# The low part of some weight pieces made by an adding DMA in place of a VectorE subtraction

## The chip, the cores and the metric

The kernel runs on one core of a Trainium2 chip. The metric is the device time of one execution in microseconds (us), the median of several runs. The engines of the core are named as in the profile: PE (TensorE, with PEld for its weight loads), DVE (VectorE), ACT (ScalarE), POOL (GpSimd) and SP (SyncE, which here only issues DMAs).

## What is computed

One decoder layer in float32 on 256 tokens of width 2048: a SwiGLU feed-forward, a token mixer (selected sparse attention beside a gated recurrence), and a second feed-forward, with a layer norm after each. The change is in the feed-forwards' input product `h @ w_in`:

```
D_MODEL = 2048
SEQ = 256
D_FF = (8 * D_MODEL // 3 + 255) // 256 * 256
...
def swiglu(h, w_in, w_out):
    a, b = jnp.split(h @ w_in, 2, axis=-1)
    return (jax.nn.silu(a) * b) @ w_out
...
h = layer_norm(DN_ALPHA * h + 0.5 * swiglu(h, ffn1_w_in[l], ffn1_w_out[l]), ln1_g[l], ln1_b[l])
...
h = layer_norm(DN_ALPHA * h + merged @ w_out[l], ln2_g[l], ln2_b[l])
h = layer_norm(DN_ALPHA * h + 0.5 * swiglu(h, ffn2_w_in[l], ffn2_w_out[l]), ln3_g[l], ln3_b[l])
```

`D_FF` is 5632, so `w_in` is 2048 x 11264.

## The kernel before

**Split operands.** TensorE multiplies in the rounded type `float32r`. So every operand is split into a high part h (the value rounded, by ScalarE, line 157) and a low part l = w - h (by VectorE, line 158), and a product is three matmuls: xh with wh, xh with wl, xl with wh (`three`, lines 521 to 523). The weights are streamed once, and each must be loaded, split and used.

**Pieces.** All weights form one list of pieces, in the order in which TensorE uses them. A piece is 128 partitions by 1024 columns (`PIECE`). Class `Weights` walks this list with three cursors: `load_to` issues the loads on SP's queue, `split_to` makes h and l, `unit` hands the columns to TensorE. Each time TensorE's program comes to a new piece, `unit` calls `load_to` for up to `AHEAD + LOADS` = 4 + 5 pieces ahead and `split_to` for up to `AHEAD` = 4 pieces ahead, and makes one step of the background work (`bg.step`: gates, norms, row loads). This sets the program's order alone. In time, what holds loads and splits back are the buffers: a plain piece is loaded into one of five raw buffers (tag `raw`), which is free again when its split is done, and h and l of each piece lie in one of five pairs (tags `wh`, `wl`, `HL_BUFS`), which is free when TensorE has used it. PE, SP and POOL run in the order of the program; the order on DVE and ACT is planned by the framework's scheduler.

**Blocks of the input product.** A feed-forward's input product has 22 blocks of 512 columns (256 of a, 256 of b), in three segments of 8, 8 and 6 (`SEGS`). After each segment comes the output product of its columns (32, 32 and 24 plain pieces). The first block of each feed-forward is made of 8 plain pieces (`PLAIN_PLAN`). The other 21 follow `FAST_PLAN`, 12 pieces: in each half of the block a plain piece ("c"), then two pieces of a fast product (a Strassen-like scheme with sums of weights), a second plain piece, and two more fast pieces:

```
c  p1q3  p2  c  q5p7  q4p6   c  p1q3  p2  c  q5p7  q4p6
```

A plain piece is 12 matmuls of 512 columns; p2 is 6 matmuls of 256 columns, the other three are 12 of 256 columns each (`blockF`). The four fast pieces of a half are made from one load of 1 MB (tag `rf`, two buffers) by sums on VectorE (`operand`, lines 128, 132 and 135); the last of them, q4p6, frees the rf buffer.

**Gates.** At a block's end, `gate` forms silu(a) * b in a buffer z (two of them); eight pieces later (four at a segment's end) TensorE transposes it (line 758).

**POOL** does little: the row loads of the norms' gains and biases (line 486), a few small instructions of the norms, and the low parts of eight pieces just ahead of the first two norms (`W.spare`).

Of the kernel before, what the change touches and what calls it, by code (L numbers as in the profile page):

```python
# [8 lines left out]
F32 = mybir.dt.float32  # L9
F32R = mybir.dt.float32r  # L10
I32 = mybir.dt.int32
AF = mybir.ActivationFunctionType
OP = mybir.AluOpType
AX = mybir.AxisListType.X

P = 128
# [28 lines left out]
for _k, _w in (("ln1_g", NK), ("ln1_b", NK), ("ln2_g", NK), ("ln2_b", NK), ("conv_w", 4 * NR),  # L45
# [5 lines left out]
LAG = 2  # L51

U_BUFS = 49
Z_BUFS = 2
T_BUFS = 8
RAW_BUFS = 5
RAWF_BUFS = 2
WS_BUFS = 1
HL_BUFS = 5
AHEAD = 4  # L60
LOADS = 5
FAST = (False, True, False, True)
FORMS = ("p1q3", "p2", "q5p7", "q4p6")
PLAIN_PLAN = tuple(("c", k) for k in range(0, NK, 2))
FAST_PLAN = tuple(p for q in (0, 2) for p in (("c", 4 * q), ("p1q3", q + 1), ("p2", q + 1),
                                              ("c", 4 * q + 2), ("q5p7", q + 1), ("q4p6", q + 1)))
LAG_T = (8, 4)
LAG_LN = 1
LAG_LAST = 4
PIECE = 1024  # L70


class Weights:
# [5 lines left out]

    def __init__(self, nc, pool, pieces, on_piece):
        self.nc, self.pool, self.on_piece = nc, pool, on_piece
        self.fast_pool = None
        self.pieces = pieces
        self.raw = {}
        self.sums = {}
        self.hl = {}
        self.loaded = 0
        self.split = 0  # L90
        self.cur = -1
        self.spare = 0
        self.off = 0

    def key(self, i):
        ap, form = self.pieces[i]
        return id(ap) if form else i

    def size(self, i):
        ap, form = self.pieces[i]  # L100
# [2 lines left out]
    def load_to(self, i, between=None):  # L103
        nc = self.nc
        while self.loaded <= min(i, len(self.pieces) - 1):
            ap, form = self.pieces[self.loaded]
            k = self.key(self.loaded)
            if k not in self.raw:
                n = ap.shape[1]
                if form:  # L110
                    t = self.fast_pool.tile([P, 2 * PIECE], F32, name=f"rf{self.loaded}", tag="rf", bufs=RAWF_BUFS)
                else:
                    t = self.pool.tile([P, PIECE], F32, name=f"raw{self.loaded}", tag="raw", bufs=RAW_BUFS)
                nc.sync.dma_start(t[:, :n], ap)
                self.raw[k] = t
                if between:
                    between(self.loaded)
            self.loaded += 1
# [21 lines left out]
    def split_to(self, i, step=PIECE):  # L140
        nc = self.nc
        while self.split <= min(i, len(self.pieces) - 1):
            form = self.pieces[self.split][1]
            self.load_to(self.split)
            k = self.key(self.split)
            h = self.pool.tile([P, PIECE], F32R, name=f"wh{self.split}", tag="wh", bufs=HL_BUFS)
            l = self.pool.tile([P, PIECE], F32R, name=f"wl{self.split}", tag="wl", bufs=HL_BUFS)
            eng = nc.gpsimd if self.spare else nc.vector
            self.spare = max(0, self.spare - 1)
            n = self.size(self.split)  # L150
            if form:
                parts = [(self.operand(k, form), *(x[:, :n].rearrange("p (f r c) -> p f r c", r=2, c=256)
                                                   for x in (h, l)))]
            else:
                parts = [tuple(x[:, q:min(n, q + step)] for x in (self.raw[k], h, l)) for q in range(0, n, step)]
            for src, hp, lp in parts:
                nc.scalar.activation(hp, src, AF.Copy)  # L157
                self.last = eng.tensor_tensor(lp, src, hp, op=OP.subtract)  # L158
            self.hl[self.split] = (h, l)
            if form in (None, FORMS[-1]):  # L160
                del self.raw[k]
            self.split += 1

    def unit(self, n):
        if self.cur < 0 or self.off == self.size(self.cur):
            self.hl.pop(self.cur, None)
            self.cur += 1
            self.off = 0
            self.load_to(self.cur + AHEAD + LOADS)
            self.split_to(self.cur + AHEAD)  # L170
            self.on_piece()
        h, l = self.hl[self.cur]
        o = self.off
        self.off += n
        assert self.off <= self.size(self.cur)
        return h[:, o:o + n], l[:, o:o + n]
# [49 lines left out]
def tile_layer(ctx, tc, x_fm, x_tm, pos, f1a, f1o, wA, wki, wB, lru, wab, wrb, wo, f2a, f2o,  # L226
               cols_d, ln1_g, ln1_b, ln2_g, ln2_b, ln3_g, ln3_b, out):
    nc = tc.nc
# [6 lines left out]
    def name(s):  # L235
        count[0] += 1
        return f"{s}{count[0]}"
# [7 lines left out]
    def T1(s="t"):  # L245
        return pool.tile([P, S], F32, name=name(s), tag="t", bufs=T_BUFS)
# [7 lines left out]
    def MM():  # L254
        return psum.tile([P, 512], F32, name=name("mm"), tag="mm", bufs=4)
# [6 lines left out]
    pieces = []  # L262

    def plain(aps):
        for ap in aps:
            for o in range(0, ap.shape[1], PIECE):
                pieces.append((ap[:, o:min(ap.shape[1], o + PIECE)], None))

    def ffn_pieces(fa, fo):
        for b0, b1 in SEGS:  # L270
            for n in range(b0, b1):
                ap = {}
                for f, k in FAST_PLAN if n else PLAIN_PLAN:
                    if f == "c":
                        pieces.append((fa[n][:, k * 512:k * 512 + PIECE], None))
                    else:
                        if k not in ap:
                            ap[k] = fa[n][:, k * 2048:(k + 1) * 2048]
                        pieces.append((ap[k], f))
            for nb in range(4):  # L280
                plain([fo[nb][:, 2 * b0 * 512:2 * b1 * 512]])
# [8 lines left out]
    for i in range(NR + LAG):  # L290
        if i < NR:
            plain([wB[RX + i], wB[RG + i]])
        if i >= LAG:
            g, c = divmod(i - LAG, TPG)
# [216 lines left out]
    def blockF(x, forms):  # L511
# [3 lines left out]
        c = [MM(), MM()]  # L515
# [8 lines left out]

        plan = FAST_PLAN if forms else PLAIN_PLAN
        seen = set()
        last = {f: i for i, (f, k) in enumerate(plan)}
        top = max(last["c"], last.get("p2", 0)), max(last["c"], last.get("q4p6", 0))
        for i, (form, k) in enumerate(plan):
# [202 lines left out]
    def ffn(x, forms, ln):  # L732
        def gate(c, e, g, i, lag):

            z = W.fast_pool.tile([P, 4 * S], F32, name=name("z"), tag="z", bufs=Z_BUFS)
            z4 = z.rearrange("p (j c) -> p j c", j=4)
# [27 lines left out]
        for s, (b0, b1) in enumerate(SEGS):  # L764
            g = [None] * (2 * (b1 - b0))
            for n in range(b0, b1):
                c, e = blockF(x, forms if n else None)
                task = gate(c, e, g, 2 * (n - b0), LAG_T[n == b1 - 1])
                next(task)
                bg.add("gate", task)  # L770
            if s == len(SEGS) - 1:
                new_stats()
                ln.prepare()
            out_product(g, s == len(SEGS) - 1 and ln)
# [189 lines left out]
    for j in range(NK):  # L964
# [3 lines left out]
        d = u[:, (j % 2) * S:(j % 2 + 1) * S]  # L968
# [45 lines left out]
    for j in range(NR + LAG):  # L1014
# [14 lines left out]
        if j >= LAG:  # L1029
            i = j - LAG  # L1030
            g, c = divmod(i, TPG)
# [6 lines left out]
            r, t = T1(), T1()  # L1038
# [11 lines left out]
    for j in range(NK):  # L1050
# [3 lines left out]
        d = u[:, (j % 2) * S:(j % 2 + 1) * S]  # L1054
# [98 lines left out]
```

## Time and profile before

| | us |
|---|---|
| median of 3 runs (2454.38 to 2456.43) | 2454.38 |
| the profiled execution, its time | 2456.76 |
| the profiled execution, its span (the stretch that the profile covers) | 2455.0 |
| PE busy | 2422.3 |
| DVE busy | 1867.1 |
| ACT busy | 1352.1 |
| POOL busy | 49.0 |
| HBM read | 458.87 MB, 188 GB/s over the span with what is written |

How to read the profile: busy times are of one execution. Groups of instructions are given as line, engine, operation, tile written <- tiles read, partitions x elements, count | busy us, mean ns | idle time of the engine just before them and what ended it. In waits the columns are total us, number, longest. In the strips each digit is the busy share of one of 40 equal slices, in tenths. A matmul's own duration is longer than the distance between two matmuls, since they are pipelined: counts and distances tell TensorE's pace, not mean durations. The columns of a window are its limits, its length, the busy time and count of PE, PEld, DVE, ACT and POOL, the granted clock of TensorE, the DMA engines' busy share, and GB/s. In the chain of work that ended last, each row is a start, a duration and what ran.

### The profile page before, as it was taken

The numbers are of one execution on the slowest core, as the hardware profiler recorded it, in microseconds if no ns is written. First come the engines' busy times: TensorE is split into PE (matmuls) and PEld (weight loads), VectorE is DVE, ScalarE is ACT, GpSimd is POOL, SyncE is SP. The second block draws the span as 40 slices with busy tenths as digits, with TensorE's granted clock in tenths as the row PEclk, the third lists the DMA queues.
The fourth block names the chain that finished last, engine by engine and source line by source line (L and its number), as shares of the span: only waits on it lengthen the run. The fifth ranks groups of instructions, "written<-read, shape, count | busy, mean of one in ns | idle before, by whom it ended". The sixth has DMA issues, their size and how long they took to land.

```text
span 2455.0 us, 35892 instructions
## 1 busy us (share of the span) xinstructions
PE 2422.3 (99%) x13980; PEld 2108.8 (86%) x13980; DVE 1867.1 (76%) x2570; ACT 1352.1 (55%) x1825; POOL 49.0 (2%) x76
## 2 busy tenths in 40 slices
PE   8999999999999999999999999999999999999997
PEld 7887888888878778889999988887888888888886
DVE  8995799669956676655788875655999589956985
ACT  6654465446535455544688874444665356544652
POOL 0000000000010000000000000002000000000001
PEclk9999999999999999999999999999999999999999
DMA  7556555555566554455556555566455655566553
GB/s 263 214 186 205 178 200 217 179 187 202 192 183 192 171 159 146 154 185 181 186 181 189 183 194 188 188 185 203 171 198 197 187 189 191 198 195 218 205 194 112
DMA packets 117658, 463.30 MB, mean 189 GB/s; under 512 B 13264, under 2 KB 13264, under 8 KB 106736
## 3 DMA queue, kind: packets, MB, share of 16 engines
q1 hardware_dynamic: 115488, 454.61, 56.1%
q0 software_dynamic: 2000, 6.41, 0.9%
q8 instruction: 109, 1.79, 0.3%
q14 instruction: 61, 0.50, 0.1%
HBM read 458.87 MB, written 2.10 MB: 188 GB/s over the span
## 4 chain that ended last, share of the span: by engine, by line
PE 95%; DVE 3%; DMA 1%; issue 0%; POOL 0%; ACT 0%; SPq 0%; POOLq 0%; ACTq 0%; DVEq 0%
PE mm L502 11%; PE mm L577 10%; PE mm L579 10%; PE mm L578 10%; PE mm L522 9%; PE mm L523 9%; PE mm L521 9%; PE mm L503 5%; PE mm L1005 4%; PE mm L1004 4%; PE mm L1003 4%; PE bp L521 3%; PE bp L523 3%; PE bp L522 3%; DVE wl L158 1%; PE bp L758 1%
## 5 line engine op out<-in xcount | busy, mean ns | idle before, releaser
L158 DVE TENSOR_TENSOR wl<-raw,wh 128x1024 fp32r<-128x1024 f32 (+2 forms) x690 | 829.6, 1204 | 479.0 <-ACT wh L157 476.6
L157 ACT ACTIVATE wh<-raw 128x1024 fp32r<-128x1024 f32 (+3 forms) x698 | 730.6, 1048 | 688.1 <-PE mm L579 373.6
L157 ACT ACTIVATE wh<-rf 128x1024 fp32r<-128x1024 f32 (+1 forms) x252 | 229.1, 913 | 215.8 <-PE mm L523 117.4
L577 PE MATMUL mm<-wh,g 128*128 128x512 f32 x704 | 278.8, 396 | 0.0
L578 PE MATMUL mm<-wl,g 128*128 128x512 f32 x704 | 278.3, 395 | 0.0
L579 PE MATMUL mm<-wh,g 128*128 128x512 f32 x704 | 278.3, 395 | 0.0
L158 DVE TENSOR_TENSOR wl<-rf,wh 128x1024 fp32r<-128x1024 f32 (+1 forms) x252 | 261.8, 1039 | 14.6 <-ACT wh L157 14.5
L521 PE MATMUL mm<-wh,xs 128*128 128x512 f32 (+1 forms) x536 | 193.9, 362 | 7.1 <-ACT wh L157 7.1
L522 PE MATMUL mm<-wl,xs 128*128 128x512 f32 (+1 forms) x536 | 194.0, 362 | 1.3 <-DVE wl L158 1.3
L523 PE MATMUL mm<-wh,xs 128*128 128x512 f32 (+1 forms) x536 | 193.9, 362 | 0.0
L522 PE MATMUL mm<-wl,hs 128*128 128x512 f32 (+1 forms) x536 | 192.9, 360 | 1.0 <-DVE wl L158 0.9
L521 PE MATMUL mm<-wh,hs 128*128 128x512 f32 (+1 forms) x536 | 192.9, 360 | 0.0
L523 PE MATMUL mm<-wh,hs 128*128 128x512 f32 (+1 forms) x536 | 192.7, 359 | 0.0
L502 PE MATMUL mm<-hs,wh 128*128 128x512 f32 x528 | 190.1, 402 | 0.0
L1005 PE MATMUL mm<-hs,wl 128*128 128x256 f32 x640 | 180.0, 281 | 0.0
L1004 PE MATMUL mm<-hs,wh 128*128 128x256 f32 x640 | 180.0, 281 | 0.0
L1003 PE MATMUL mm<-hs,wh 128*128 128x256 f32 x640 | 180.0, 281 | 0.0
L579 PEld LDWEIGHTS mm<-wh,g 128*128 128x128 f32 x704 | 132.2, 188 | 32.3
L577 PEld LDWEIGHTS mm<-wh,g 128*128 128x128 f32 x704 | 132.2, 188 | 31.5
L578 PEld LDWEIGHTS mm<-wl,g 128*128 128x128 f32 x704 | 132.2, 188 | 31.3
L503 PE MATMUL mm<-hs,wl 128*128 128x256 f32 x528 | 148.7, 282 | 0.0
L523 PE MATMUL bp<-wh,sl 128*128 128x256 f32 x504 | 141.3, 280 | 0.0
(255 smaller groups left out, 5201.9 us busy)
## 6 DMA issues: line engine op xcount, KB each, us to landing
raw<-wB SPq DMA_DIRECT2D x144, 512.0 KB, 3.8
raw<-f1a SPq DMA_DIRECT2D x92, 512.0 KB, 6.4
raw<-f2a SPq DMA_DIRECT2D x92, 512.0 KB, 5.9
raw<-f1o SPq DMA_DIRECT2D x88, 512.0 KB, 3.7
raw<-f2o SPq DMA_DIRECT2D x88, 512.0 KB, 3.7
rf<-f1a SPq DMA_DIRECT2D x42, 1024.0 KB, 4.9
rf<-f2a SPq DMA_DIRECT2D x42, 1024.0 KB, 5.0
raw<-wA SPq DMA_DIRECT2D x64, 512.0 KB, 3.7
```

Source lines behind the costliest of these rows:

```text
L157: nc.scalar.activation(hp, src, AF.Copy)
L158: self.last = eng.tensor_tensor(lp, src, hp, op=OP.subtract)
L502: T.matmul(ps, w[0], x.rearrange("p a t -> p (a t)"), start=first, stop=False)
L521: T.matmul(ps, xh, w[0], start=start, stop=False)
L522: T.matmul(ps, xh, w[1], start=False, stop=False)
L523: T.matmul(ps, xl, w[0], start=False, stop=stop)
L577: T.matmul(ps[t], xh, wh, start=k == 0, stop=False)
L578: T.matmul(ps[t], xh, wl, start=False, stop=False)
L579: T.matmul(ps[t], xl, wh, start=False, stop=k == n - 1)
L1003: T.matmul(ps[:, :S], w[0], x[:, 0], start=first, stop=False)
L1004: T.matmul(ps[:, :S], w[0], x[:, 1], start=False, stop=False)
L1005: T.matmul(ps[:, :S], w[1], x[:, 0], start=False, stop=last)
```

## The change

In each half of a fast block the second plain piece becomes form "d" (entry "add" in the list): two of the four plain pieces of a block. Such a piece leaves `load_to` and `split_to`. It is made by a new function, `sum_next`, that `unit` calls at each new piece: the raw load goes to SP's queue, ScalarE writes l = -w (rounded) and h = w (rounded), and a DMA on POOL's queue adds w from HBM onto l. Its h and l lie in tiles of their own (tags `ah`, `al`), of which there is one each. The function is called for the next adding piece once TensorE's program has come past the one before, and at most `ADD_LEAD` = 9 pieces ahead. To make room, the z buffers go from two to one and the raw buffers from five to four; `LOADS` goes from 5 to 4.

```diff
-Z_BUFS = 2
+Z_BUFS = 1
 T_BUFS = 8
-RAW_BUFS = 5
+RAW_BUFS = 4
 RAWF_BUFS = 2
 WS_BUFS = 1
 HL_BUFS = 5
 AHEAD = 4
-LOADS = 5
+LOADS = 4
+ADD_LEAD = 9
...
 FAST_PLAN = tuple(p for q in (0, 2) for p in (("c", 4 * q), ("p1q3", q + 1), ("p2", q + 1),
-                                              ("c", 4 * q + 2), ("q5p7", q + 1), ("q4p6", q + 1)))
+                                              ("d", 4 * q + 2), ("q5p7", q + 1), ("q4p6", q + 1)))
...
+        self.adds = deque(i for i, p in enumerate(pieces) if p[1] == "add")
+        self.last_add = -1
...
-            if k not in self.raw:
+            if form != "add" and k not in self.raw:
...
             form = self.pieces[self.split][1]
+            if form == "add":
+                self.split += 1
+                continue
             self.load_to(self.split)
...
+    def sum_next(self):
+
+        nc = self.nc
+        if self.adds and self.cur > self.last_add and self.adds[0] <= self.cur + ADD_LEAD:
+            i = self.last_add = self.adds.popleft()
+            ap = self.pieces[i][0]
+            t = self.pool.tile([P, PIECE], F32, name=f"raw{i}", tag="raw", bufs=RAW_BUFS)
+            nc.sync.dma_start(t, ap)
+            h = self.fast_pool.tile([P, PIECE], F32R, name=f"ah{i}", tag="ah", bufs=1)
+            l = self.fast_pool.tile([P, PIECE], F32R, name=f"al{i}", tag="al", bufs=1)
+            nc.scalar.activation(l, t, AF.Copy, scale=-1.0)
+            nc.scalar.activation(h, t, AF.Copy)
+            nc.gpsimd.dma_start(l, ap, accum_op=OP.add)
+            self.hl[i] = (h, l)
+
     def unit(self, n):
         if self.cur < 0 or self.off == self.size(self.cur):
             self.hl.pop(self.cur, None)
             self.cur += 1
             self.off = 0
+            self.sum_next()
             self.load_to(self.cur + AHEAD + LOADS)
             self.split_to(self.cur + AHEAD)
             self.on_piece()
...
-                    if f == "c":
-                        pieces.append((fa[n][:, k * 512:k * 512 + PIECE], None))
+                    if f in "cd":
+                        pieces.append((fa[n][:, k * 512:k * 512 + PIECE], None if f == "c" else "add"))
...
         plan = FAST_PLAN if forms else PLAIN_PLAN
         seen = set()
+        plan = [("c" if f == "d" else f, k) for f, k in plan]
```

More of the change, by code (lines that the diff above doesn't have):

```diff
@@ L96, in key @@
         ap, form = self.pieces[i]
-        return id(ap) if form else i
+        return id(ap) if form in FORMS else i
     def size(self, i):
@@ L107, in load_to @@
             k = self.key(self.loaded)
-            if k not in self.raw:
+            if form != "add" and k not in self.raw:
                 n = ap.shape[1]
-                if form:
+                if form in FORMS:
                     t = self.fast_pool.tile([P, 2 * PIECE], F32, name=f"rf{self.loaded}", tag="rf", bufs=RAWF_BUFS)
```

## The prediction

> **What bounds the kernel now.** I read the page's busy times and strips first, then the windows of one product stage each, the waits of TensorE, and the chain where TensorE did wait.
>
> ```profile
> PE 2422.3 (99%) x13980; PEld 2108.8 (86%) x13980; DVE 1867.1 (76%) x2570; ACT 1352.1 (55%) x1825; POOL 49.0 (2%) x76
> PE   8999999999999999999999999999999999999997
> DVE  8995799669956676655788875655999589956985
> ```
>
> ```profile
> 195.00:285.00 90.00, 90.00 (x401) 73.07 (x400) 50.38 (x50) 34.95 (x36) 0.00 (x0) 1.00 0.59 182
> 290.00:462.00 172.00, 172.00 (x1069) 153.12 (x1068) 163.55 (x200) 103.23 (x126) 0.00 (x0) 1.00 0.55 196
> ```
>
> The second window row is the stage that the change touches (input products with fast forms). Columns: length, then PE, PEld, DVE, ACT, POOL busy, granted clock, DMA share, GB/s. VectorE is busy 163.55 of 172 us there, 95%, and still TensorE is busy 172.00 of 172: VectorE is nearly full, but TensorE sets the pace. So relief of VectorE pays only where TensorE is seen to wait for it:
>
> ```profile
> PE mm L521 <- ACT wh L157: 7.1, 2, 6.3
> PE mm L522 <- DVE wl L158: 2.2, 4, 0.8
> PEld bp L758 <- DVE z L752: 1.9, 2, 1.0
> ```
>
> ```profile
> 72.60 1.06 ACT wh L157
> 73.68 1.23 DVE wl L158
> ...
> 87.57 1.15 DVE wl L158
> 88.76 0.50 PE mm L522
> ...
> 193.79 0.69 DVE z L752
> 194.53 0.66 PE bp L758 x4
> ...
> 332.22 0.44 PE bp L758 x4
> 353.69 0.44 PE bp L758 x4
> ...
> 1778.95 1.15 DVE wl L158
> 1780.14 0.50 PE mm L522
> ...
> 2365.47 0.44 PE bp L758 x4
> ...
> 2437.52 0.79 POOL s L634
> ```
>
> Waits are given as sum, times, longest. The 7.1 us is the first weights of all, before any adding piece. What is left is 2.2 us on low parts (at 88 us, where a backlog of VectorE that starts at 72.6 ends, and the like at 1780 in the second feed-forward) and 1.9 us on two gates like the one at 194.53. Together 4.1 us: that is all that relief can win. The transposes at 332.22 and 353.69 are one block apart and give its period: 21.47 us.
>
> **What the change removes.** Two low parts a block, 42 blocks (21 with forms in each feed-forward), 84 in all:
>
> ```profile
> L158 DVE TENSOR_TENSOR wl<-raw,wh 128x1024 fp32r<-128x1024 f32 x664 | 809.9, 1221 | 465.1 <-ACT wh L157 462.7
> L157 ACT ACTIVATE wh<-raw 128x1024 fp32r<-128x1024 f32 x672 | 713.1, 1062 | 685.7 <-PE mm L579 373.6 <-issue 99.7 <-PE mm L502 78.4
> ```
>
> VectorE loses 2 x 1.22 = 2.44 us of 20.4 a block (163.55 / 172 x 21.47), to 18.0, 84%. Worth on the path: between 0 and 4.1 us. I take 2: both backlogs see at most two or four such pieces before they end, the gates have other VectorE work in front of them.
>
> **What it adds to ScalarE.** One activation more for each such piece (l and h instead of h): 84 x 1.06 us, which takes ScalarE from 12.9 us a block (103.23 / 172 x 21.47) to 15.0, 70%. Its cover is that it already waits for TensorE's releases (373.6 us in the row above). Without that cover it would be 89 us.
>
> **What it adds to the path: the round of one pair of tiles.** The tiles ah and al exist once. So the next l cannot be written before TensorE has finished the piece before it with adds, and five pieces later TensorE wants the new one. That round is the core of the case. The time it has: between the two adding pieces stand q5p7, q4p6, a plain piece, p1q3 and p2, by the code 42 matmuls of 256 columns and 12 of 512. A block has 84 and 48. Counting a 256 as half, 33 of 90 parts of (21.47 - 0.44) us are **7.7 us**; the round that holds the four transposes has 0.44 more, **8.15**. (The time of the adding piece itself is not in it.)
>
> The time it needs: l (1.06 us), three hand-overs of some 0.03 to 0.1 (72.60 + 1.06 to 73.68 is one), a share of what ScalarE has in hand, 0.3 as an estimate (its 60% times half an instruction), so **1.5 us and the adding transfer X**. It decides at X = 6.2 and 6.65 us. No adding transfer is in this trace; its neighbours are:
>
> ```profile
> raw<-wB SPq DMA_DIRECT2D x144, 512.0 KB, 3.8
> raw<-lru SPq DMA_DIRECT2D x8, 256.0 KB, 2.8
> gr<-ln_g POOLq DMA_DIRECT2D x12, 256.0 KB, 7.0
> DMA to landing us min/median/max: 3.3/7.0/10.1
> ```
>
> ```profile
> gr<-ln_g POOLq DMA_DIRECT2D x4, 256.0 KB, 3.4
> rf<-f2a SPq DMA_DIRECT2D x1, 1024.0 KB, 4.9
> ...
> br<-ln_b POOLq DMA_DIRECT2D x1, 256.0 KB, 6.0
> ```
>
> The first of these two fences is the whole run (the minimum and maximum belong to gr), the second the stretch 2236 to 2256, where POOL's rows fall into gaps of SP's traffic, and one issue at 1725 beside SP's loads. A quiet POOL transfer of 256 KB lands in 3.4 us against 2.8 on SP's queue: 0.6 more. **Below**: it moves 512 KB like a plain load, 3.8 + 0.6 = 4.4 us. **Between**: it must read what stands in l as well as w, so it moves like a load of 1 MB, 4.9 + 0.6 = 5.5. **Above**: it is caught by SP's loads as the rows of 6.0 and 7.0 were, 2.6 to 3.6 more than the quiet 3.4, so 8.1 to 9.1. I take **5.5**, as the quiet ends are the nearest if the DMA engines are quiet then, which they should be:
>
> ```profile
> DMA  7000000094999999900000009499899960000000
> ...
> rf<-f1a SPq DMA_DIRECT2D x3, 1024.0 KB, 4.9
> ```
>
> ```profile
> 324.78 0.33 SPq L114 DMA_DIRECT2D rf<-f1a  x1
> 325.15 0.91 SPq L114 DMA_DIRECT2D raw<-f1a  x2
> ...
> 335.32 0.33 SPq L114 DMA_DIRECT2D rf<-f1a  x1
> ```
>
> The strip is 320 to 347 us, 0.68 us a digit: SP's loads come in one burst each half block, some 6 us full and 5 us empty. The burst starts when q4p6's low part has freed its rf buffer. Now its start (324.78) falls some 2 us before the end of what will be an adding piece (a plain piece, q5p7 and q4p6, 24 of 90 parts or 5.6 us, stand between that end and the transposes at 332.22: 326.6), which would be the worst place. But the adding pieces leave the rotation of five wh/wl buffers, so the five reach one piece further: a q4p6 is split when TensorE has done the q4p6 before it (12 of 90 parts, 2.8 us after the end of the adding piece), no longer after the plain piece that follows. 2.8 + 1.06 + 1.22 us of split and some waiting put the burst at 5 to 6 us after that end, and its 6 us are over at 11 to 12. The transfer runs from 1.5 to 7.0, and the next one starts 10.7 (half a block) later. They touch, but hardly share.
>
> So each round needs 1.5 + 5.5 = 7.0 of 7.7 or 8.15 us: **hidden, with 0.7 and 1.15 us to spare.** That cover is thin. With X at 8.1 to 9.1 the rounds lack 1.9 and 1.45, or 2.9 and 2.45 us, and 42 of each are 141 to 225 us.
>
> **The rest, costed at nothing.** The 84 transfers read 44 MB more, 0.5 MB in each empty part of the strip above; without those gaps they are what the upper end of X prices. The raw load of an adding piece goes to SP in place of the old one: same bytes, far ahead. POOL's queue is empty between the norms, so only the next adding transfer and the row loads of gains stand behind a waiting one; those of the last norm, now from 2237.14 on, go after the last adding transfer (5.6 us before the transposes at 2365.47, and 1.2 for l: 2361), and are first used by the final norm, whose first step starts at 2437.52. Without that cover of 76 us, seven of them in a row are 7 x 0.54 us of issue and one landing. One z buffer: a gate starts at its block's end, and the transposes that free z run at the eighth of the block's twelve pieces, 33 of 90 parts or 7.7 us before. Four raw buffers and four loads ahead: in the plain stages a piece lasts 12 x 0.234 = 2.8 us, so four hold 11.2 us against 3.8 + 1.06 + 1.22 of load and split; only the two starts, where a load is waited for, could feel it.
>
> **Sum.** The profiled run took 2456.8 us (span 2455.0 and 1.8 around it); 2 less are 2454.8. The median of the runs is 2.4 below the profiled one, so **2452.4**. The likeliest case's own range is 2449 to 2457.
>
> **Rivals.**
> - *The adding transfer lands late* (slower). From X above 6.2 on, each round stops TensorE at the first matmul with l, and since al is free only after it, nothing catches up. At X = 7.2, halfway to the row of 8.1: 42 x (1.0 + 0.55) = 65 us, 2518. For it speak the 7.0 median of POOL's rows, and the thin cover; against it the quiet 3.4 and the shift of the burst. At the upper bound of 9.1 it is 225 us, 2677. Chance 0.38.
> - *VectorE holds up POOL's issue* (slower). The quiet POOL rows lie where VectorE is half idle:
>
> ```profile
> 2236.00:2246.00 10.00, 10.00 (x44) 8.05 (x43) 5.43 (x7) 3.48 (x4) 3.68 (x7) 1.00 0.51 161
> 2237.14 0.54 POOL L486 DMA_DIRECT2D gr<-ln_g  x1 [511.29 <-PE mm L579]
> ```
>
> In the fast blocks VectorE will be 84% busy. If POOL's issue had to wait for one or two of its instructions, 1.22 or 2.44 us, X would be 6.7 or 7.9: 42 x (0.5 + 0.05) = 23, or 42 x (1.7 + 1.25) = 124 us, so 2475 or 2576. No row shows such a wait, nor excludes it. Chance 0.04. The Trainium skill's page "SBUF — State Buffer" (section "SBUF: two separate sides", and "Who interferes with whom") warns of it for this change: a DMA issued from GpSimd cannot write its descriptors while VectorE runs in a mode that takes the port pair they share. It adds that tensor_tensor, which is nearly all of VectorE's work here, has no such mode; by that half the rival falls away.
> - *Fewer buffers cost at the starts* (slower). The backlog that ends at 88.76 begins with a load that lands at 72.6; if such a load comes one plain piece later in each feed-forward, 2 x 2.8 = 5.6 us, that is 2460. For it speaks that SP then has one load less out; against it that VectorE has 2.44 us less to do in every block of that stretch. Chance 0.04.
> - *More than the waits* (faster by over 0.2%). All 4.1 us of the waits go and the rest of a split with them (1.06 us): 2449. For it, that VectorE's backlog also delays releases; against it, that TensorE's waits are all that the end can see. Chance 0.06.
>
> **How the numbers follow.** Forecast 0.48, late transfer 0.38, issue 0.04, starts 0.04, more than the waits 0.06. A measurement of this kernel tells some 0.2%, 4.9 us, from no change: so faster 0.06, same 0.48, slower 0.46. The range runs from 2449 to 2565: below it lie 0.04, above it the late half of the transfer's case, some 0.14.
>
> **What will show it.** In the changed profile: the landing of the transfers on al (5.5, decides at 6.2); whether TensorE has a wait for al at all; VectorE at 84% in the fast windows; SP's burst 5 to 6 us after an adding piece ends. The forecast is wrong if the block period rises above 21.47 us, and by how much, times 42, says how wrong.

## The result, and the profile after

| | before | after |
|---|---|---|
| median of 4 runs side by side, us | 2454.38 (2453.45 to 2456.43) | 2468.02 (2467.36 to 2470.14) |
| ratio to before, 95% interval | | 1.0056 (1.0038 to 1.0073) |
| the profiled execution, its time | 2456.76 | 2468.03 |
| its span | 2455.0 | 2466.3 |

The changed kernel is 13.6 us slower, 0.56%. In the profiled executions the difference is 11.3 us; the other 2.4 are the distance between before's profiled execution and its median. The working below closes the 11.3.

The page after, its busy times, two strips and the share of POOL's DMA queue (q0):

```profile
PE 2424.0 (98%) x13980; PEld 2105.1 (85%) x13980; DVE 1775.8 (72%) x2486; ACT 1423.7 (58%) x1909; POOL 122.1 (5%) x160
DVE  8885688668857676655788875655988478856875
DMA  9876788678766554455555565565787678767873
q0 software_dynamic: 14096, 50.45, 11.8%
```

84 subtractions have left VectorE (2570 to 2486), 84 activations have come to ScalarE, 84 DMAs to POOL. TensorE's busy time is nearly unchanged (2422.3 before): the time has gone into gaps. In the stretch 290 to 462 there are hardly any:

```profile
290.00:462.00 172.00, 171.52 (x1066) 152.14 (x1066) 147.20 (x185) 113.02 (x139) 12.12 (x14) 1.00 0.81 235
```

TensorE is busy 171.52 of 172 us, with VectorE at 147.20 / 172 = 86%; the missing half microsecond lies at the end of the stretch (433 and 444 us). From 290 to 410 us TensorE is busy all the time. The adding transfers themselves, in the view of the tile al, and the waits of TensorE that name them:

```profile
L183 POOL DMA_DIRECT2D al<-f1a x42: 857/866/929, 29.2 to 656.3; - x42
L183 POOL DMA_DIRECT2D al<-f2a x42: 853/867/940, 1730.3 to 2366.0; - x42
...
DMA to landing us min/median/max: 5.4/5.7/9.5
```

```profile
PEld mm L545 <- DMA al<-f2a: 6.3, 7, 2.1
PEld mm L545 <- DMA al<-f1a: 5.1, 6, 2.5
```

The median of 5.7 us is below the 6.2 at which a round becomes late. But 13 of the 84 rounds were late, each by 0.3 to 2.5 us. (By the distances between the starts of TensorE's matmuls in the trace they cost 9.3 us in all.) They are not spread over the run: three belong to the third transfer of the first feed-forward and to the third and fourth of the second, the other ten to the last four transfers of a segment. In the chain:

```profile
51.29 1.07 ACT al L181
52.65 8.96 DMA al<-f1a
61.66 0.50 PE mm L545
...
1763.51 8.08 DMA al<-f2a
1771.63 0.50 PE mm L545
...
1775.63 8.93 DMA al<-f2a
1784.60 0.50 PE mm L545
...
2348.60 0.44 PE bp L782 x4
...
2372.83 10.23 DMA raw<-f2o
2384.25 1.23 DVE wl L165
...
2389.19 0.65 PE bp L782 x4
...
2457.28 1.62 POOLq L1173
```

Here the adding transfers take 8.1 to 9.0 us and TensorE starts within 0.1 us of their landing. What runs beside the first of them (50 to 62 us, all issues of that stretch; the last number is the median landing):

```profile
y<-x_tm SPq DMA_DIRECT2D x4, 256.0 KB, 9.8
...
rf<-f1a SPq DMA_DIRECT2D x1, 1024.0 KB, 7.5
...
al<-f1a POOLq DMA_DIRECT2D x1, 512.0 KB, 9.0
```

In the steady stretch 320 to 347 us an al lands in 5.6 us between SP's bursts; at the start SP's loads run at the same moment as the adding transfer, and all are late.

The first late round costs more than its wait. Just behind it the granted clock of TensorE is halved (the last three columns are clock, DMA share and GB/s):

```profile
63.60:65.60 2.00, 2.00 (x6) 1.61 (x5) 1.15 (x2) 0.89 (x3) 0.00 (x0) 0.50 1.03 407
```

By the trace's records the clock is 0.50 from 62.64 to 66.05 us, which costs half of these 3.4 us, 1.7 us. In the kernel before it is 1.00 in the same window. Behind the other late rounds it stays at 1.00.

The same three marks of before (the transposes of the last full block, the last transposes, and the last row of the chain, which begins 0.03 us before POOL's last step; the last store is issued when that step is over) give the balance:

```profile
2344.01 0.44 PE bp L758 x4
...
2382.03 0.44 PE bp L758 x4
...
2449.91 1.63 POOLq L1149
```

| us after before's | block's transposes | last transposes | last row | end of span |
|---|---|---|---|---|
| after | +4.6 | +7.2 | +7.4 | +11.3 |

So there are losses in three places: before 2344, between there and the last transposes, and after the last row. The last is the clearest: from the last row's start to the end of the span it is 5.1 us before and 9.0 after, with the same work in it. The middle one begins with a load that took 10.23 us; POOL's queue in that place:

```profile
2365.96 0.87 POOL L183 DMA_DIRECT2D al<-f2a  x1 [10.00 <-ACT al L181]
2366.51 0.89 POOL L509 DMA_DIRECT2D gr<-ln_g  x1
...
2373.96 0.55 POOL L509 DMA_DIRECT2D br<-ln_b  x1 [3.34 <-DMA al<-f2a]
```

```profile
raw<-f2o SPq DMA_DIRECT2D x6, 512.0 KB, 8.8
...
gr<-ln_g POOLq DMA_DIRECT2D x4, 256.0 KB, 9.9
br<-ln_b POOLq DMA_DIRECT2D x4, 256.0 KB, 10.1
```

The second fence is the stretch 2352 to 2380: the last norm's eight row loads (2 MB) go out together behind the last adding transfer, beside SP's loads of the output product's first pieces, which need 8.8 us, where the median of these loads in the kernel before is 3.7.

### The profile page after: what moved, and what is told of

Same layout as the page of the kernel before. It is cut to its first block, busy times and chain, and to the rows that moved or that the text cites. A ratio compares the mean times of both kernels' runs of the same rounds, so it can differ in the third digit from the quotient of the medians.

```text
span 2466.3 us, 36018 instructions
## 1 busy us (share of the span) xinstructions
PE 2424.0 (98%) x13980; PEld 2105.1 (85%) x13980; DVE 1775.8 (72%) x2486; ACT 1423.7 (58%) x1909; POOL 122.1 (5%) x160
## 3 DMA queue, kind: packets, MB, share of 16 engines
q0 software_dynamic: 14096, 50.45, 11.8%
## 4 chain that ended last, share of the span: by engine, by line
PE 93%; DMA 4%; DVE 1%; ACT 1%; issue 0%; POOL 0%; POOLq 0%; SPq 0%; ACTq 0%; DVEq 0%
PE mm L525 10%; PE mm L601 10%; PE mm L603 10%; PE mm L602 10%; PE mm L545 9%; PE mm L546 8%; PE mm L544 8%; PE mm L526 5%; PE mm L1029 4%; PE mm L1027 4%; PE mm L1028 4%; PE bp L546 3%; PE bp L544 3%; PE bp L545 3%; DMA al<-f1a 2%; DMA al<-f2a 2%
## 5 line engine op out<-in xcount | busy, mean ns | idle before, releaser
L165 DVE TENSOR_TENSOR wl<-raw,wh 128x1024 fp32r<-128x1024 f32 (+3 forms) x606 | 728.3, 1203 | 490.0 <-ACT wh L164 488.8
L164 ACT ACTIVATE wh<-raw 128x1024 fp32r<-128x1024 f32 (+2 forms) x614 | 641.5, 1046 | 720.1 <-PE mm L603 347.8
L165 DVE TENSOR_TENSOR wl<-ws,wh 128x1024 fp32r<-128x1024 f32 x84 | 102.9, 1225 | 94.5 <-ACT wh L164 93.0
L544 PE MATMUL bp<-wh,sh 128*128 128x256 f32 x504 | 140.6, 279 | 0.0
L545 PE MATMUL bp<-wl,sh 128*128 128x256 f32 x504 | 140.6, 279 | 0.0
L544 PE MATMUL mm<-wh,xs 128*128 128x512 f32 (+1 forms) x368 | 127.1, 345 | 6.6 <-ACT wh L164 6.6
L181 ACT ACTIVATE al<-raw 128x1024 fp32r<-128x1024 f32 x84 | 88.8, 1057 | 71.2 <-PE mm L545 68.2
L545 PE MATMUL mm<-wl,xs 128*128 128x512 f32 (+1 forms) x368 | 127.0, 345 | 0.8 <-DVE wl L165 0.8
```

Source lines behind the costliest of these rows:

```text
L544: T.matmul(ps, xh, w[0], start=start, stop=False)
L545: T.matmul(ps, xh, w[1], start=False, stop=False)
```

## The experiments

The theory: VectorE's relief is worth some us; it is eaten by (a) rounds that are late where SP's loads lie differently from the steady blocks, (b) the row loads, which now go out at the wrong place, (c) a longer end, which has to do with the number of DMAs on POOL's queue. The rivals: smaller buffers cost the time; the adding transfer costs it everywhere; the end is a matter of the norm itself. Each ratio is against the kernel before on the same chip, with the 95% interval.

**The relief alone, and the transfer without the add.** Two kernels. In the first the DMA on POOL is taken away, all else stays; in the second it stays, but copies. Both leave the low part of these pieces out of the product.

```diff
-            nc.gpsimd.dma_start(l, ap, accum_op=OP.add)
```

> The changed kernel without the 84 transfers (l stays -w, so the low part is left out of the result); buffers, loads and ScalarE's work as in the changed kernel. Theory A (relief is worth the 4 us of TensorE's waits on VectorE, buffers cost nothing): 2450 to 2452, last drain 2.2 us after POOL's last work. Rival C (four raw buffers, four loads ahead and one z buffer cost at the starts): 2457 or more, with TensorE waiting for weights before 95 us and between 1745 and 1800.

```diff
-            nc.gpsimd.dma_start(l, ap, accum_op=OP.add)
+            nc.gpsimd.dma_start(l, ap)
```

> The changed kernel with the transfer onto l as a plain one instead of an adding one: l becomes w, so the low part is left out of the result. Bytes from HBM are the same, what stands in l is not read. Theory A (the rounds are late by the second read): packets of 0.16 in place of 0.33 us, landing at 4.4 in place of 5.7 us, no waits for al outside the start, and 9 us of such waits become 3 or less: 2462. POOL's last drain keeps its 6.6 us. Rival (the rounds are late by SP's loads in the same ring of engines, whatever the transfer reads): waits for al stay at 7 us or more, 2466 to 2468.

Without the transfer: 2451.34 us (before 2456.39), 0.9979 (0.9970 to 0.9989), so 5.0 us faster. The relief is real. The marks of its chain and its span:

```profile
2339.59 0.44 PE bp L781 x4
...
2377.60 0.44 PE bp L781 x4
...
2445.46 1.63 POOLq L1172
```

It is 4.4 us ahead at each mark and at the end of its span (2450.6). By the starts of every block's transposes in the two traces it wins this in four steps: 0.9 us at the third block of the first feed-forward, 0.7 at its eighth, 2.2 at the second and third block of the second, 0.7 at its eighth. These are the places where TensorE waited for VectorE before.

With a copying transfer: 2462.07 us, 1.0025 (1.0013 to 1.0036), span 2460.3. Its landings and its chain:

```profile
DMA to landing us min/median/max: 3.8/3.9/7.7
```

```profile
2340.79 0.44 PE bp L782 x4
...
2380.70 0.66 PE bp L782 x4
...
2448.80 1.63 POOLq L1173
```

It lands in 3.9 us, and two waits for al are left in the list instead of 13 (1.2 us together by the matmuls' distances). At the block's transposes it is 3.2 us ahead of before, 1.2 less than without a transfer. So the late rounds come with the add, not with the transfer as such: 5.7 against 3.9 us, and by the busy share of POOL's DMA queue over the 0.9% of before, (11.8 - 0.9)% x 2466.3 / 84 = 3.2 us of all 16 engines for each transfer, against (7.0 - 0.9)% x 2460.3 / 84 = 1.8. The Trainium skill's page "Collectives: The Full Stack" (section "The bandwidth ceiling: the fold count and why AG ≠ RS ≠ AR") says of the add in a ReduceScatter between cores that it reads two sources where an AllGather's copy reads one, and so comes to half the rate. The DMA packets of 4 KB in the two traces are near that, though this is no collective (median 0.33 us adding, 0.17 copying).

The expectation missed the end: it is not shorter without adds but longer, 11.5 us from the last row to the end of the span (before 5.1, the changed kernel 9.0). So what is paid there goes by the number of DMAs, not by what they add. That the time is just the 2462 expected is partly luck: the rounds gained more and the end lost more.

**The end: a drain ahead of the last norm.** The last row of the chain is a drain on POOL; the row gives its line alone, and its time only up to the end of POOL's last step. In the trace's records this drain ends 6.58 us after POOL's last step in the changed kernel, 2.21 before. If it pays for all DMAs that POOL ever issued, an earlier drain takes most of it out of the end.

```diff
             self.rows = [(row(self.g, nb, "gr"), row(self.b, nb, "br")) for nb in range(4)]
+            G.drain()
```

> The changed kernel with one drain instruction on POOL's queue right behind the row loads of the last norm, about 2380 us, where POOL has nothing else to do until 2444. Theory A (POOL's last instruction, a drain that took 8.2 us in the changed kernel and 3.8 before, clears something for each of POOL's DMAs, 6.6 against 2.2 us after POOL's last work): the end falls back to 2.2 us after POOL's last work, the time to 2464 (4 us less). Theory B (that drain waits for something that only happens at the end): 2468, unchanged, and the last drain still 6.6 us after POOL's last work.

Measured: 2465.33 us, 1.0037 (1.0023 to 1.0050), span 2462.5, 3.8 us shorter than the changed kernel's. Its last row:

```profile
2457.40 1.62 POOLq L1174
```

From there to the end it is 5.1 us again, as before. The last drain ends 0.07 us after POOL's last work. The mark itself has not moved (2457.28 without the drain): the gain is all at the end. The earlier drain takes 14.9 us of POOL's time, from 2372.7 to 2387.6 (the last row load lands within it, at 2383.0), and nobody waits for POOL there.

**The end from the other side.** The kernel before, with 84 small plain loads of 64 KB on POOL's queue, two for each fast block, that nobody reads:

```diff
+        self.odd = False
...
+                if self.pieces[self.cur][1] in ("p1q3", "q5p7"):
+                    self.odd = not self.odd
+                    if self.odd:
+                        t = self.fast_pool.tile([P, 128], F32, name=f"sd{self.cur}", tag="sd", bufs=1)
+                        self.nc.gpsimd.dma_start(t, self.pieces[self.cur][0][:, :128])
```

> The kernel before, with 84 small plain loads (128 x 128, 64 KB) on POOL's queue into a tile that nobody reads, two in each fast block. Theory A (each POOL DMA leaves something that the last drain clears, whatever it moved): POOL's last drain ends 6.6 to 9.1 us after POOL's last work in place of 2.2, and the time rises by 4 to 6.5 us with nothing else changed before it. Rival (only adding or large transfers leave it): last drain at 2.2 us, time within 1 us of before.

Measured: 2462.66 us (before 2455.49), 1.0027 (1.0018 to 1.0037), with no adding DMA and no change in any block. By the medians that is 7.2 us, a little over the 4 to 6.5 expected. Its span is 2460.3, and its last row:

```profile
2448.87 1.62 POOLq L1155
```

The row starts 1.0 us earlier than before's, and yet the span is 5.3 us longer: 11.4 us of end, as in the copying kernel with its 84 DMAs of 512 KB. So the end depends on how many DMAs POOL issued, not on their size or on the number of their packets (32 and 144 each), and nearly all of them were long over by then. From the drain: 2.21 us at 26 DMAs, 9.07 at 110 in both kernels, 82 ns for each; with 84 of the 110 adding, 6.58, or 52 ns for each of these. Why adding ones cost less stays open. The drain decides only when it is over later than what SP does behind the last store: of the 5.1 us that the end takes before, a drain can win nothing.

**The rows.** In each feed-forward the row loads go out before the last segment's blocks:

```diff
         for s, (b0, b1) in enumerate(SEGS):
             g = [None] * (2 * (b1 - b0))
+            if s == len(SEGS) - 1:
+                ln.prepare()
...
             if s == len(SEGS) - 1:
                 new_stats()
-                ln.prepare()
```

> The changed kernel with the eight row loads of the last norm put ahead of the last segment in the program instead of behind it, so that they no longer queue behind the last adding transfers. Theory A (the 2 MB of rows, let loose at 2366 us, hold up the first loads of the output product, and the last gate with them): the load that took 10.2 us lands in 4 to 6, the last transposes come 2.4 us earlier, 2465.6. Rival (the two last adding transfers themselves hold that load up): 2468, unchanged.

Measured: 2465.20 us, 1.0040 (1.0025 to 1.0055), span 2462.6. In the stretch 2352 to 2380 SP's loads of the output product land normally again, and the chain's first two marks are 38.46 us apart (38.02 before, 40.59 in the changed kernel):

```profile
raw<-f2o SPq DMA_DIRECT2D x7, 512.0 KB, 4.1
```

```profile
2347.32 0.44 PE bp L782 x4
...
2385.78 0.44 PE bp L782 x4
...
2453.64 1.62 POOLq L1174
```

Loss (b) is 2.1 us (2.4 expected). The end is still 9.0 us long (2462.6 - 2453.64), so this and the drain add up.

**The smaller buffers.** The two pieces become plain again; z, raw buffers and `LOADS` stay cut, and no piece is an adding one:

```diff
-                                              ("d", 4 * q + 2), ("q5p7", q + 1), ("q4p6", q + 1)))
+                                              ("c", 4 * q + 2), ("q5p7", q + 1), ("q4p6", q + 1)))
```

> The changed kernel without any adding piece (all four plain pieces of a block are split as before), so only the smaller buffers are left: four raw buffers, four loads ahead, one z buffer. Theory A (the run without transfers was faster by relief of VectorE, buffers are worth nothing either way): the kernel before, within 1.5 us, with TensorE's waits at 88, 194, 1780 and 1902 us as before. Rival (the smaller buffers themselves made that run faster, by letting the first loads of x land sooner): 3 us or more below the kernel before.

Measured: 2456.61 us against 2456.27, 1.0003 (0.9994 to 1.0012). On balance the buffers cost nothing and win nothing. TensorE's waits were expected to be those of before, and they are not: those for low parts are longer (2.2 us before), and those for gates (1.9 us before) are gone.

```profile
PE mm L545 <- DVE wl L165: 3.1, 4, 1.1
```

**Adds in the steady blocks only**, with the rows early and a drain behind the last segment's blocks:

```diff
-                        pieces.append((fa[n][:, k * 512:k * 512 + PIECE], None if f == "c" else "add"))
+                        add = f == "d" and n != b1 - 1 and n > (1 if fa is f1a else 2)
+                        pieces.append((fa[n][:, k * 512:k * 512 + PIECE], "add" if add else None))
```

> The changed kernel with adding pieces only where rounds were in time: not in the last block of a segment, nor in the first fast block of the first feed-forward and the first two of the second (66 of 84 stay); with the norm's rows ahead of the last segment and a drain on POOL once the last adding transfer has been issued. Theory A: waits for al below 1.5 us, last drain done with POOL's last work, so what is left is the relief that the run without transfers showed, less the share of the pieces taken out: 1.5 to 4.5 us faster than the kernel before on the same chip. Rival (late rounds go with the blocks that begin and end a run of adding pieces, wherever that is): the waits move to the new first and last blocks, 4 us or more, no gain.

Measured: 2461.77 us, 1.0023 (1.0015 to 1.0032): no gain over before, where a gain was expected. The rounds at the segments' ends are no longer late, but the late ones at the start have moved with it:

```profile
PEld mm L546 <- DMA al<-f1a: 2.9, 1, 2.9
...
PEld mm L546 <- DMA al<-f2a: 2.2, 1, 2.2
```

They are now the second transfers of the block with which the adds begin. Behind the second of them the granted clock is 0.50 from 1806.85 to 1810.27 us, as behind the first late round of the changed kernel. A further 2.5 us are waits for low parts between 1750 and 1830 us, where the kernel without a transfer has none: VectorE has these subtractions back. So the late rounds at the start move with the block in which a feed-forward's adds begin. It is not so at every beginning: the runs of adding pieces behind an output product have no late round at their start, in this kernel or in the changed one. And at the segments' ends nothing moved: the blocks that now come last are in time.

**Two al tiles**, so that a round has a whole block half more. The lead goes from 9 to 11 pieces, and the next adding piece may be made once the one before the last is used. First with nothing else, then with the rows early and the drain:

```diff
-ADD_LEAD = 9
+ADD_LEAD = 11
...
-        self.last_add = -1
+        self.last_add = self.before_last = -1
...
-        if self.adds and self.cur > self.last_add and self.adds[0] <= self.cur + ADD_LEAD:
-            i = self.last_add = self.adds.popleft()
+        if self.adds and self.cur > self.before_last and self.adds[0] <= self.cur + ADD_LEAD:
+            i = self.adds.popleft()
+            self.before_last, self.last_add = self.last_add, i
...
-            l = self.fast_pool.tile([P, PIECE], F32R, name=f"al{i}", tag="al", bufs=1)
+            l = self.fast_pool.tile([P, PIECE], F32R, name=f"al{i}", tag="al", bufs=2)
```

> The changed kernel with two al tiles instead of one (ah stays single) and the call for an adding piece up to two pieces earlier (lead 11 for 9), so that l is written and added a round ahead; rows and drain as in the changed kernel. Theory A (late rounds come from the single al: 1.5 us and the transfer have only 7.7 or 8.15 us): no waits for al, 9 us less than the changed kernel, some 2459 to 2460, with POOL's last drain and the late rows left. Rival (the transfers hold up SP's loads and so the splits, whenever they run): TensorE waits for wh or wl in place of al, 2464 or more.

```diff
         for s, (b0, b1) in enumerate(SEGS):
             g = [None] * (2 * (b1 - b0))
+            if s == len(SEGS) - 1:
+                ln.prepare()
...
             if s == len(SEGS) - 1:
                 new_stats()
-                ln.prepare()
+                G.drain()
```

> The run with two al tiles, the norm's rows ahead of the last segment, and a drain on POOL once the last adding transfer has been issued, all 84 adding pieces kept. Theory A (the three costs are separate and add up): the relief alone is left, as in the run without transfers, 3 to 5 us faster than the kernel before on the same chip. Rival (they cover each other): 2456 or more.

Measured: 2464.52 us, 1.0032 (1.0021 to 1.0043), and 2458.79 us, 1.0011 (1.0002 to 1.0020). No wait of TensorE for al is left in either list, although al lands later (median 7.1 and 7.2 us): the round is longer. Both still lose some 6 us at the start of the first feed-forward, most of it in one wait of TensorE for a gate. The wait and the chain of the first of them:

```profile
PEld bp L783 <- DVE z L777: 4.7, 1, 4.7
```

```profile
56.27 0.33 SPq L118
...
56.65 10.29 DMA y<-x_tm
```

This load is the token rows that the kernel reads there, not a weight piece. It takes 10.28 us in the second too. ScalarE stands still for it, and behind it, ahead of the gate's silu, it has the two activations of the next adding piece. Behind TensorE's wait the granted clock is 0.50 from 71.67 to 78.49 us. The load alone does not make the loss: in the kernel with few adds below, which has no adding transfer in this stretch, one such load takes nearly as long, and TensorE has no wait for a gate.

```profile
55.75 9.80 DMA y<-x_tm
```

The 5.7 us between the two kernels are what the row loads and the end cost. So two tiles cure the late rounds, and adding pieces still cost time in this place; the kernel whose adds begin behind it (the last one below) does not lose there. How the loss divides between the DMA engines, which are full, and the order of the work on ScalarE is not shown. That is why both expectations were missed: the waits for al went, but only part of the time (1.0032 in place of 1.0056 with nothing else changed).

**Fewer adds**, in the kernel with two tiles, rows early and drain: first only where VectorE had its backlogs, then everywhere but the first blocks of the first feed-forward:

```diff
-                        pieces.append((fa[n][:, k * 512:k * 512 + PIECE], None if f == "c" else "add"))
+                        add = f == "d" and (5 if fa is f1a else 1) <= n <= 7
+                        pieces.append((fa[n][:, k * 512:k * 512 + PIECE], "add" if add else None))
```

> Two al tiles, norm's rows ahead, drain on POOL, and adding pieces only in blocks that run up to a place where TensorE waited for VectorE in the kernel before: blocks 5 to 7 of the first feed-forward (the gate at 194) and 1 to 7 of the second (1775 to 1798 and the gate at 1902), 20 of 84. Theory A (relief is worth something only there, and the start of the first feed-forward is where DMA engines have nothing left for adding transfers): 2.5 to 4 us below the kernel before. Rival (relief works through all blocks): no better than the run with all 84 and two al tiles, 2457 to 2459.

```diff
-                        pieces.append((fa[n][:, k * 512:k * 512 + PIECE], None if f == "c" else "add"))
+                        add = f == "d" and (4 if fa is f1a else 1) <= n
+                        pieces.append((fa[n][:, k * 512:k * 512 + PIECE], "add" if add else None))
```

> As the run with few adding pieces, but with them in all blocks save the first three fast ones of the first feed-forward (78 of 84). Theory A (78 transfers in steady blocks cost nothing with two al tiles; only those at the start of the first feed-forward did): as the run with few, within 1 us, 2.5 to 4 us below the kernel before. Rival (each transfer costs a little, by DMA traffic): 1.5 us or more above the run with few.

Measured: 2455.97 us (20 adding pieces), 0.9998 (0.9990 to 1.0007), which is no gain where 2.5 to 4 us were expected; and 2453.62 us (78 adding pieces), 0.9991 (0.9982 to 1.0000), 2.65 us faster than before by the medians, within the 2.5 to 4 expected for it. The marks of the second:

```profile
2339.36 0.44 PE bp L784 x4
...
2377.37 0.44 PE bp L784 x4
...
2445.23 1.62 POOLq L1177
```

They are 4.6 to 4.7 us ahead of before's, and the end is 5.2 us long (span 2450.4). But 2.0 us of this lead are there at the end of the first block, before any adding piece: this execution lacks a stretch of half clock that before's has at 17 us (below). The other 2.7 agree with the medians. So with two al tiles, a start behind the full stretch, the rows early and the drain, the change brings about half of the 5.0 us that the kernel without the transfer wins. It is the fastest version that computes everything, but its interval reaches 1.0000. The intervals of these two overlap, so they do not show that the larger number of adding pieces is what wins.

## Why the prediction was wrong

The forecast was "hidden", 2452.4 us, with 2449 to 2457 for that case; it is 2468. The time lies within the whole range only because that reached into the late transfer's case. By the profiled executions, with the terms that the runs give:

| term | predicted, us | measured, us | from |
|---|---|---|---|
| relief of VectorE | -2 (0 to -4.1) | -4.4 | the kernel without the transfer |
| rounds of ah and al | 0 | +9.0 | block's transposes 2348.60, against 2339.59 without the transfer |
| the last rounds and the row loads | 0 | +2.6 | from there to the last transposes, 40.59 against 38.01 us |
| the last norm | 0 | +0.2 | to the last row, 68.09 against 67.86 us |
| POOL's end | 0 | +3.9 | 9.0 against 5.1 us |
| sum | -2 | +11.3 | |

The profiled executions differ by 1 to 2 us at the end of the first block already, before any add, so single terms of the table are not sharper than that. The granted clock explains most of it: it is 0.50 from 17.0 to 20.4 us before and from 17.3 to 20.7 without the transfer, and 1.00 there in the changed kernel and in the one whose adds start late; half the clock for 3.4 us is 1.7 us. This is not the change's doing: the kernel with few adds, without an adding piece up to there either, has the 0.50. Counted from the last matmul of the first block (34.03 us before, 32.43 in the changed kernel, 34.77 without the transfer) the relief is 5.2 us, near the 5.0 of the medians, and the rounds cost 11.4: 9.3 in waits, 1.7 in half clock behind the first of them, and 0.4 that is not placed.

**What held.** The adding transfer was taken at 5.5 us and has a median of 5.7. In the steady blocks it is hidden, as forecast: 71 of 84 rounds are in time, and the block period is 21.45 us (transposes at 312.17 and 333.62 us). So the sign that the prediction named, a block period above 21.47, did not show in these blocks, and all the time was lost elsewhere. The shift of SP's burst held: the rf load was put at 5 to 6 us after the end of the adding piece, and here it is, 5.7 us after that end (317.31, where the next l starts):

```profile
323.02 0.33 SPq L118 DMA_DIRECT2D rf<-f1a  x1
323.40 0.46 SPq L178 DMA_DIRECT2D raw<-f1a  x1
```

VectorE stands at 86% (84 predicted), ScalarE at 113.02 / 172 = 66% (70 predicted). The one z buffer, the four raw buffers and the added activations at nothing were right: the kernel with only the cut buffers is within 0.1%.

**The first failing step: "hidden, with 0.7 and 1.15 us to spare", for all rounds.** The cover was worked out in one steady stretch, 320 to 347 us, and multiplied over 42 blocks. Its condition, "if the DMA engines are quiet then", was looked at in that stretch alone. Where the adds of a feed-forward begin, and at the ends of the segments, SP's loads do not yet, or no longer, lie in the gap that the strip showed; there the adding transfer shares the engines with them. The three late ones at the beginnings took 8.1 to 9.0 us, what the upper bound of 8.1 to 9.1 had priced, the ten at the segments' ends 6.7 to 7.7. (The longest, 9.5 us, are first transfers of a segment, for which nobody waits yet.) The price by that bound, 1.45 to 2.9 us a round, was of the right size for the rounds at the beginnings (1.7 to 2.5 us by the list of waits; those at the segments' ends lost 0.3 to 0.9). What was wrong is how many: none or all 84, where it was 13. The case between was in no rival, and neither was the half clock behind a wait. That the add is the cause is shown by the copying transfer, which brings the loss before 2344 from 9.0 to 1.2 us; that the beginning does it for the first three, by the late rounds moving along with it. For the ten at the ends the trace shows only that SP's queue fills 19 to 26% of the engines' time while they run, 5 to 18% between 297 and 410 us; no run moved those loads.

**The second: "the rest, costed at nothing", in two places.** The row loads were put at 2361 and found at 2366.5, and their cover of 76 us for the use of the rows holds. But the cover was asked of the rows only, not of what they push aside: 2 MB at once beside the loads that the output product begins with, 2.1 us. And POOL's queue was looked at for what stands behind a waiting instruction, not for what 84 more DMAs leave at the end: the drain stands in the views only as a line number, and the step did not ask what closes the span after the last row, though the last row of the chain, 2449.91 + 1.63, ends 3.5 us before the span does. 3.9 us, shown by the drain that takes it away and by 84 small loads that bring it about.

**The third: the size of the relief.** 2 us were taken of a bound of 4.1; it was 4.4 in the profile and 5.0 in the runs. In the kernel without the transfer, TensorE's 1.9 us of waits for gates have gone from the list, and of the 2.2 us for low parts 1.0 is left. So 3.1 of the 4.1 us went. Why is only in part shown: the gates' waits are gone with the smaller buffers alone, too, where no low part has left VectorE, so the argument that the gates have other VectorE work in front of them is not refuted. Against that kernel it is the waits for low parts that fall, from 3.1 to 1.0 us. The 1.3 us between 3.1 and 4.4 are no wait that the list shows, and lie within what executions differ by.

**The rivals.** The late transfer was right in its mechanism, in 13 rounds. That VectorE holds up POOL's issue did not happen: in the steady stretch the first packet of each adding transfer leaves 1.57 to 1.59 us after the issue starts, with VectorE at 86%. Where it leaves more than 0.1 us later (up to 4.4 us; 13 of the 84, most of them not the late rounds), SP's loads keep the DMA engines 93% busy or more until then, which explains it without VectorE. The Trainium skill's page "SBUF — State Buffer" (section "Who interferes with whom") says that tensor_tensor has no 2-port mode; that POOL's issue is not held up in the steady stretch agrees with it. Fewer buffers at the starts: nothing, shown. More than the waits: the relief by itself, 4.4 to 5.0 us, comes near its price of 4.1 + 1.06, and the other terms take it back.

## What to carry to other kernels

A cover that a steady stretch shows holds in that stretch: before it is multiplied, the first rounds and the last ones have to be asked what else the DMA engines carry there, and a load that is moved is to be asked what it pushes aside, too. A transfer that adds occupies the DMA engines nearly twice as long as a copy (3.2 against 1.8 us here), so its tile needs a second buffer where the round has less than that to spare; in this case the second buffer alone won back less than half of the loss. And what closes the span after the last row of the chain is a term of its own; if DMAs are issued from POOL, a drain put where POOL has nothing to do keeps their price out of the end.

## What the runs showed of the hardware

- The end of the program pays for the DMAs that POOL issued during the whole run: the drain is over 2.21 us after POOL's last step at 26 DMAs, 9.07 and 9.08 at 110 plain ones (84 of them of 512 KB or of 64 KB), 6.58 where 84 of the 110 add. A drain placed earlier leaves 0.07 us.
- An adding DMA from HBM onto SBUF of 512 KB lands in 5.4 to 5.9 us in the steady blocks, against 3.8 to 4.0 for the copy on the same queue, and its packets take 1.9 times as long (0.328 against 0.174 us).
- After a wait of TensorE of 2.5 us the granted clock was 0.50 for 3.4 us, after one of 4.7 us for 6.8 us; after waits of 1.7 and 2.1 us in the changed kernel it stayed at 1.00. It did not follow every long wait: with the adds in the steady blocks only it stayed at 1.00 after one of 2.9 us.
